# Feed-forward matrices as 2x2 blocks with seven products, in one layer of a hybrid encoder on one core

## The chip, the core and the metric

The kernel runs on one of the eight cores of a Trainium2 chip. A core has five engines that run side by side and are tied together by semaphores: TensorE (PE in the profile) multiplies matrices, with weight loads on a row of their own (PEld); VectorE (DVE) does elementwise work and reductions; ScalarE (ACT) does elementwise functions and casts; GpSimd (POOL) does elementwise work on SBUF only; SyncE (SP) here issues DMA transfers. SBUF is the memory on the core with 128 partitions, PSUM the accumulators that TensorE writes. The metric is the device time of one execution in microseconds, and the median over runs is compared.

## The reference, cut to what matters

One encoder layer on 512 tokens of width 2048, in float32: a normalised input projection that feeds two recurrent head groups, an output projection, cross-attention into 256 memory tokens, a feed-forward part with hidden width 8192, and a last normalisation. The change is in the feed-forward part:

```python
hn = _rmsnorm(h, norm_mlp[l])
h = h + jnp.square(jax.nn.relu(hn @ mlp_w_up[l])) @ mlp_w_down[l]
return _rmsnorm(h, norm_final)
```

`mlp_w_up` is 2048 x 8192 and `mlp_w_down` is 8192 x 2048.

## The kernel before, in words

Activations lie transposed in SBUF: a tile holds 128 features by 512 tokens, so the residual stream `h` is 16 tiles (`hres`). A matrix product is made of matmuls of a 128x128 block of weights against a 128x512 tile. To keep float32 precision every operand is cut into a rounded high part and the rest (`split`, L131 to L136: ScalarE casts the high part, VectorE subtracts it from the source for the low part), and each block costs three matmuls, high by high, high by low and low by high (`gemm`, L152 and L124). Weights come in pieces of 128x1024 (eight blocks, 512 KB) through `wload`: a raw tile of three (`wraw`), split into one of two pairs (`whi`, `wlo`).

The first stages (projections, recurrent heads, keys) are ordered by a planner in the kernel itself (L248); these lines the change does not touch. From the value projection on, the kernel is written in plain order, and the framework sets the order of instructions on each engine, inserts the semaphores and gives tiles their places. There follow the value stage (vp, vo), the output projection (op), the scores and softmax (sc), the attention product (at), which also adds into `hres` and makes the split, gain-scaled input of the feed-forward part (`nh_`, `nl_`, 32 tiles), and the feed-forward part itself.

This runs in eight rounds. A round makes eight 128-row tiles of the hidden activations: each is 16 blocks x 3 matmuls (48), read from PSUM by ScalarE (relu), multiplied by the normaliser `rstd` and squared by VectorE, and split into `uh`, `ul`. Then for each of the 16 output tiles 8 blocks x 3 matmuls (24) multiply the round's hidden tiles, and VectorE adds the result from PSUM to `hres` (L1340). So hidden activations never leave SBUF, and GpSimd has no part. At the end the residual is squared, summed and normalised, and written out.

Of the kernel before, what the change touches and what calls it, by code (L numbers as in the profile page):

```python
# [9 lines left out]
F32 = mybir.dt.float32  # L10
F32R = mybir.dt.float32r
AF = mybir.ActivationFunctionType
ALU = mybir.AluOpType
# [4 lines left out]
P = 128  # L18
T = 512
M = 256  # L20
KD = 16
# [52 lines left out]
def build(tc, I, out):  # L74
    nc = tc.nc
    V, S, GP, PE = nc.vector, nc.scalar, nc.gpsimd, nc.tensor
    es = ExitStack()

    pc = es.enter_context(tc.tile_pool(name="pc", bufs=1))
    pd = es.enter_context(tc.tile_pool(name="pd", bufs=1, space=DRAM))  # L80
    ps = es.enter_context(tc.tile_pool(name="ps", bufs=1, space=PSUM))
    pw = es.enter_context(tc.tile_pool(name="pw", bufs=1))
# [17 lines left out]
    def col(name, i=0):  # L100
        o, w = PRM[name]
        return prm[:, o + i:o + i + 1]
# [17 lines left out]
    def psb(nm, tag="mx", bufs=2):  # L120
        return tile_of(ps, [P, 512], F32, tag, nm, bufs)
# [4 lines left out]
    def rsq(o, x, scale, eps):  # L126
        S.activation(o, x, AF.Ln, bias=eps, scale=scale)
        S.activation(o, o, AF.Exp, scale=-0.5)

    def split(src, hi, lo, gain=None):  # L130
        if gain is None:  # L131
            S.copy(hi, src)  # L132
            V.tensor_tensor(out=lo, in0=src, in1=hi.bitcast(F32), op=ALU.subtract)  # L133
# [204 lines left out]
    def act_tile(nm, dt=F32R):  # L338
        return tile_of(pa, [P, 512], dt, "act", nm, 32)
# [5 lines left out]
    rstd = pc.tile([P, T], F32, name="rstd")  # L345
# [4 lines left out]
    cnt = [0]  # L350
# [25 lines left out]
    raws, halves, used = {}, {}, set()  # L376
# [31 lines left out]
    acc = tl("r")  # L408
# [759 lines left out]

    pm_cm.__exit__(None, None, None)
    pq_cm.__exit__(None, None, None)  # L1170
    pl = es.enter_context(tc.tile_pool(name="pl", bufs=1, reuse_waits="tile"))

    def btile(nm):
        return pl.tile([P, 512], F32R, tag="actb", name=nm, bufs=32)

    def sl2(w=512):
        cnt[0] += 1
        return pl.tile([P, 512], F32, tag="sl", name=f"sl{cnt[0]}", bufs=3)[:, 0:w]

    hres = [pl.tile([P, T], F32, tag=f"h{k}", name=f"h{k}", bufs=1) for k in range(16)]  # L1180

    oh, ol = [], []
    for n in range(KD):
        r = pl.tile([P, 512], F32, tag="slr", name=f"mx{n}", bufs=3)
        nc.sync.dma_start(r, mixd[n])
        hi, lo = btile(f"oh{n}"), btile(f"ol{n}")
# [54 lines left out]
    acc = pl.tile([P, T], F32, tag="acc", name="acc1", bufs=1)  # L1241
    hh_, hl_ = [], []
    for n in range(KD):
        xr = sl2()
# [16 lines left out]
    V.tensor_scalar(out=nrcol, in0=rcol, scalar1=-1.0, scalar2=None, op0=ALU.mult)  # L1261


    phi = [btile(f"phi{m}") for m in range(8)]
    plo = [btile(f"plo{m}") for m in range(8)]
    for g in range(2):
        pts = [psb(f"sc{g}_{t}", ("mm", "mm", "mg", "mg")[t]) for t in range(4)]
        for n2 in range(8):
            cnt[0] += 1
            raw = pw.tile([P, 1024], F32, tag="wraw", name=f"kqr{cnt[0]}", bufs=NWR)  # L1270
            for i in range(2):
                nc.sync.dma_start(raw[:, i * 512:(i + 1) * 512], KQd[2 * n2 + i][:, g * 512:(g + 1) * 512])
            wh = pw.tile([P, 1024], F32R, tag="whi", name=f"kqh{cnt[0]}", bufs=NWS)
            wl = pw.tile([P, 1024], F32R, tag="wlo", name=f"kql{cnt[0]}", bufs=NWS)
            split(raw, wh, wl)
            for i in range(2):
                n = 2 * n2 + i
                w1, w2 = wh[:, i * 512:(i + 1) * 512], wl[:, i * 512:(i + 1) * 512]
                for t in range(4):
                    a1, a2 = hh_[n][:, t * P:(t + 1) * P], hl_[n][:, t * P:(t + 1) * P]  # L1280
                    mm(pts[t], a1, w1, start=(n == 0), stop=False)
                    mm(pts[t], a1, w2, start=False, stop=False)
                    mm(pts[t], a2, w1, start=False, stop=(n == 15))
        ptr = [[None] * 2 for _ in range(2)]
        probs = []
        for t in range(4):
            for e in range(2):
                s = pts[t][:, e * M:(e + 1) * M]
                mx = pl.tile([P, 1], F32, tag="mx1", name=f"mx{g}_{t}_{e}", bufs=4)
# [3 lines left out]
                pr = pl.tile([P, 512], F32, tag="actb", name=f"pr{g}_{t}_{e}", bufs=32)[:, 0:M]  # L1293
                sm = pl.tile([P, 1], F32, tag="sm1", name=f"sm{g}_{t}_{e}", bufs=4)
                S.activation(pr, s, AF.Exp, bias=nb, scale=rcol[:, t:t + 1], accum_out=sm)
                V.reciprocal(out=sm, in_=sm)
                V.tensor_scalar(out=pr, in0=pr, scalar1=sm, scalar2=None, op0=ALU.mult)
                probs.append(pr)
        for e in range(2):
            for mt in range(2):  # L1300
                pt = psb(f"ptr{g}_{e}_{mt}")
                for t in range(4):
                    PE.transpose(pt[:, t * P:(t + 1) * P], probs[t * 2 + e][:, mt * P:(mt + 1) * P], ident)
                kk = (g * 2 + e) * 2 + mt
                S.copy(phi[kk], pt)
                V.tensor_tensor(out=plo[kk], in0=pt, in1=phi[kk].bitcast(F32), op=ALU.subtract)

    acc = pl.tile([P, T], F32, tag="acc", name="acc2", bufs=1)
    nh_, nl_ = [], []
    for n in range(KD):  # L1310
        pt = psb(f"at{n}", "mm", 2)
        gemm(pt, VOd[n // 4][:, :, (n % 4) * P:(n % 4 + 1) * P], 8, phi, plo)
        V.tensor_tensor(out=hres[n], in0=hres[n], in1=pt, op=ALU.add)
        hi, lo = act_tile(f"nh{n}"), act_tile(f"nl{n}")
        split(hres[n], hi, lo, col("norm_mlp", n))
        nh_.append(hi)
        nl_.append(lo)
        finish(n, acc)
    pt = psb("pss2")
    mm(pt, ones, acc)  # L1320
    rsq(rstd, pt, 1.0 / 2048, b_eps6)


    for e in range(8):
        uh, ul = [], []
        for i in range(8):
            pt = psb(f"up{e}_{i}", "mm", 2)
            gemm(pt, I["w_up"][e * 8 + i], KD, nh_, nl_)
            r = sl2()
            S.activation(r, pt, AF.Relu)  # L1330
            V.tensor_tensor(out=r, in0=r, in1=rstd, op=ALU.mult)
            V.tensor_tensor(out=r, in0=r, in1=r, op=ALU.mult)
            hi, lo = btile(f"uh{e}_{i}"), btile(f"ul{e}_{i}")
            split(r, hi, lo)
            uh.append(hi)
            ul.append(lo)
        for n in range(KD):
            pt = psb(f"dn{e}_{n}", "mm", 2)
            gemm(pt, I["w_dn"][e, n], 8, uh, ul)
            V.tensor_tensor(out=hres[n], in0=hres[n], in1=pt, op=ALU.add)  # L1340


    acc = pl.tile([P, T], F32, tag="acc", name="acc3", bufs=1)
    for n in range(KD):
        finish(n, acc)
    pt = psb("pss3")
# [10 lines left out]
def layout(inputs):  # L1357
# [28 lines left out]
    def put(name, arr, rows=slice(0, P)):  # L1386
        o, n = PRM[name]
        prm[rows, o:o + n] = arr
# [14 lines left out]
    for n, k in (("w0", "rwkv_w0"), ("a0", "rwkv_a0"), ("kk", "rwkv_k_k"), ("ka", "rwkv_k_a"),  # L1403
# [21 lines left out]
    d["w_up"] = tiles(a["mlp_w_up"][0])  # L1425
    wd = a["mlp_w_down"][0]
    d["w_dn"] = np.ascontiguousarray(
        wd.reshape(8, 8, P, 16, P).transpose(0, 3, 2, 1, 4).reshape(8, 16, P, 1024))
    return d


# [14 lines left out]
```

## Time and profile before

| | us |
|---|---|
| median of 3 runs (3126.75 to 3129.79) | 3126.99 |
| the profiled execution | 3125.39 |
| its span, first to last instruction | 3123.6 |
| up to the query-key fold, 0 to 1066 | 1066 |
| query-key fold (kq), value stage (vp, vo), 1066 to 1345 | 279 |
| output projection, scores, attention product, 1345 to 1703 | 358 |
| feed-forward part, 1703 to 3099 | 1396 |
| last normalisation and output, 3099 to 3124 | 25 |

In a group's row stand the line, the engine, the operation, output and inputs by the program's names, the shapes and the count; then busy time and mean nanoseconds of one, and the engine's idle time before them with what ended it. Matmuls are pipelined: a matmul's own duration (389 ns) is longer than the distance between two of them, so what a stage of matmuls costs is read from its length and their number. A line can be a helper's.

### The profile page before, as it was taken

To read this page: it belongs to the slowest core of one execution; us is meant where nothing else is said; L and a number is where in the kernel's file an instruction comes from. 1 tells how busy PE (TensorE), PEld (TensorE's weight loads), DVE (VectorE), ACT (ScalarE), POOL (GpSimd) and SP (SyncE) were. 2 spreads that over 40 slices of the span, in tenths; PEclk is the share of its full clock that TensorE was granted. 3 is DMA by queue.
4 is the path that set the end of the run, shared out by engine and by line. 5 is a ranking of instruction groups with operands and counts; after the bars stand their busy time and mean duration, and the time that the engine had idled before them with its cause. 6 is when DMAs were issued, how large, how long until landed. Compare 5 with 4: busy or idle time off the path is not lost.

```text
span 3123.6 us, 44560 instructions
## 1 busy us (share of the span) xinstructions
PE 3069.4 (98%) x18294; PEld 2529.6 (81%) x18294; DVE 1564.7 (50%) x2259; ACT 1192.9 (38%) x1568; POOL 202.5 (6%) x547
## 2 busy tenths in 40 slices
PE   8999999999999999999999999999999999999997
PEld 6878888888777898788878888888888888888885
DVE  6576666666667647434355433334333433333344
ACT  6455454454555555533244222222222222222232
POOL 0202311311311000000000000000000000000000
PEclk9999999999999999999999999999999999999998
DMA  5332423432434686853323332323333332323332
GB/s 172 105 85 78 107 80 82 110 82 80 131 88 146 192 278 218 263 174 118 105 88 95 100 96 95 99 97 95 98 98 95 99 98 95 99 97 95 99 97 95
DMA packets 203388, 360.79 MB, mean 116 GB/s; under 512 B 89064, under 2 KB 108780, under 8 KB 203184
## 3 DMA queue, kind: packets, MB, share of 16 engines
q1 hardware_dynamic: 198576, 349.55, 36.6%
q10 hardware_dynamic: 4608, 8.39, 0.7%
q8 instruction: 144, 2.36, 0.3%
q14 instruction: 60, 0.49, 0.1%
HBM read 327.06 MB, written 30.81 MB: 115 GB/s over the span
## 4 chain that ended last, share of the span: by engine, by line
PE 71%; DMA 1%; ACT 1%; DVE 1%; issue 0%; ACTq 0%; DVEq 0%; SPq 0%
PE dn L124 22%; PE up L124 22%; PE op L124 6%; PE py L248 3%; PE vo L124 3%; PE kq L248 3%; PE sc L124 3%; PE kp L248 3%; PE at L124 3%; PE vp L124 2%; DMA mx<-mixd 1%; DMA out_dram<-sl 0%; DMA wraw<-in_w_in 0%; PE rs L248 0%; PE gs L248 0%
## 5 line engine op out<-in xcount | busy, mean ns | idle before, releaser
L132 ACT CAST whi<-wraw 128x1024 fp32r<-128x1024 f32 x368 | 387.3, 1052 | 1098.0 <-PE dn L124 471.5
L133 DVE TENSOR_TENSOR wlo<-wraw,whi 128x1024 fp32r<-128x1024 f32 x368 | 450.8, 1225 | 533.7 <-ACT whi L132 532.9
L124 PE MATMUL dn<-ul,whi 128*128 128x512 f32 x1024 | 399.3, 390 | 0.0
L124 PE MATMUL up<-nl,whi 128*128 128x512 f32 x1024 | 398.8, 389 | 0.0
L124 PE MATMUL dn<-uh,wlo 128*128 128x512 f32 x1024 | 398.5, 389 | 0.0
L124 PE MATMUL dn<-uh,whi 128*128 128x512 f32 x1024 | 398.4, 389 | 0.0
L124 PE MATMUL up<-nh,whi 128*128 128x512 f32 x1024 | 398.4, 389 | 0.0
L124 PE MATMUL up<-nh,wlo 128*128 128x512 f32 x1024 | 398.4, 389 | 0.0
L248 PE MATMUL py<-xhi,whi 128*128 128x512 f32 x928 | 374.2, 403 | 13.2 <-ACT xhi L248 10.8
L248 PE MATMUL py<-xhi,wlo 128*128 128x512 f32 x928 | 371.9, 401 | 0.6 <-DVE wlo L248 0.5
L248 PE MATMUL py<-xlo,whi 128*128 128x512 f32 x928 | 371.9, 401 | 0.0
L1340 DVE TENSOR_TENSOR h<-h,dn 128x512 f32<-128x512 f32 x128 | 87.9, 687 | 400.6 <-PE dn L124 400.6
L248 DVE TENSOR_TENSOR wlo<-wraw,whi 128x1024 fp32r<-128x1024 f32 x180 | 221.6, 1231 | 132.7 <-ACT whi L248 127.8
L248 ACT CAST whi<-wraw 128x1024 fp32r<-128x1024 f32 x180 | 188.9, 1049 | 234.0 <-PE py L248 188.6
L124 PEld LDWEIGHTS dn<-ul,whi 128*128 128x128 f32 x1024 | 192.2, 188 | 42.9 <-DVE ul L133 2.9
L124 PEld LDWEIGHTS up<-nl,whi 128*128 128x128 f32 x1024 | 192.2, 188 | 40.2 <-issue 0.2
L124 PEld LDWEIGHTS up<-nh,whi 128*128 128x128 f32 x1024 | 192.2, 188 | 40.1
L124 PEld LDWEIGHTS dn<-uh,whi 128*128 128x128 f32 x1024 | 192.2, 188 | 39.9
L124 PEld LDWEIGHTS up<-nh,wlo 128*128 128x128 f32 x1024 | 192.2, 188 | 39.7 <-issue 0.2
L124 PEld LDWEIGHTS dn<-uh,wlo 128*128 128x128 f32 x1024 | 192.2, 188 | 39.5
L248 PEld LDWEIGHTS py<-xhi,whi 128*128 128x128 f32 x928 | 175.1, 189 | 52.6 <-ACT xhi L248 10.8
L248 PEld LDWEIGHTS py<-xhi,wlo 128*128 128x128 f32 x928 | 175.0, 189 | 37.7 <-DVE wlo L248 1.7
(678 smaller groups left out, 4808.6 us busy)
## 6 DMA issues: line engine op xcount, KB each, us to landing
wraw<-in_w_up SPq DMA_DIRECT2D x128, 512.0 KB, 3.6
wraw<-in_w_dn SPq DMA_DIRECT2D x128, 512.0 KB, 3.6
wraw<-in_w_in SPq DMA_DIRECT2D x118, 512.0 KB, 3.9
wraw<-in_wk SPq DMA_DIRECT2D x32, 512.0 KB, 3.7
wraw<-in_wqT SPq DMA_DIRECT2D x32, 512.0 KB, 3.9
wraw<-in_wv SPq DMA_DIRECT2D x32, 512.0 KB, 4.7
wraw<-in_wo SPq DMA_DIRECT2D x32, 512.0 KB, 3.6
wraw<-in_w_out SPq DMA_DIRECT2D x32, 512.0 KB, 3.9
```

The source lines that it names most:

```text
L124: PE.matmul(o, l, r, start=start, stop=stop)
L132: S.copy(hi, src)
L133: V.tensor_tensor(out=lo, in0=src, in1=hi.bitcast(F32), op=ALU.subtract)
L248: f(*a, **k)
L1340: V.tensor_tensor(out=hres[n], in0=hres[n], in1=pt, op=ALU.add)
```

## The change

Both feed-forward products are made by the scheme of Strassen in Winograd's form. A unit takes 256 output rows and a set of row groups (pairs of 128 input rows) and cuts weights and activations into 2x2 blocks: the weights into a11, a12, a21, a22 by halves of the output and of each input pair, the activations by halves of the pair and of the tokens (256 each). Instead of eight block products it makes seven (`product`), of these weight sides: a11; s1 = a21 + a22; s2 = s1 - a11; a11 - a21; a22; s4 = a12 - s2; a12. The activation sides are seven tiles per group (`comb`), each with its high part in columns 0 to 255 and its low part in 256 to 511, made by `place` with four subtractions on GpSimd, seven copies on ScalarE and seven subtractions on VectorE. The four weight sums of a unit are on GpSimd, the seven splits as before on ScalarE and VectorE, now of the sums too. Seven additions on VectorE put the PSUM results together in two output tiles (`c1`, `c2`, of the three `sl` tiles).

The up product has 32 units with all eight groups (blocks of 128x1024). Its outputs are scaled, clipped and squared (`square`) and written to device memory (`Ud`, 64 writes from ScalarE's queue). The down product is run after all of up, in one chunk of two groups and six chunks of five (blocks of 128x256 and 128x640), eight units each; the result of each unit is added to `hres` by GpSimd (`into`; by VectorE in the last unit). `unit` reads a group back from memory and rebuilds its seven tiles; this is placed among the units of the chunk before. The weights are laid out by block in the inputs.

Around it: pools are regrouped so that the 56 activation tiles fit, the attention stage builds the first ones in place of `nh_` and `nl_`, the softmax rows get tiles of their own, and the reloaded mixer outputs use `sl` tiles.

```diff
-        hi, lo = act_tile(f"nh{n}"), act_tile(f"nl{n}")
-        split(hres[n], hi, lo, col("norm_mlp", n))
+        g = sl2()
+        S.activation(g, hres[n], AF.Copy, scale=col("norm_mlp", n))
+        if n % 2 == 0:
+            ge = g
+        if n % 2 == 0 and n < KD - 2:
+            for i in (B11, T1):
+                place(i, n // 2, ge, None)
+        elif n % 2 == 1:
+            for i in range(2 if n < KD - 2 else 0, 7):
+                place(i, n // 2, ge, g)
...
+    def put(i, k, src):
+        t = comb[i][k]
+        S.copy(t[:, HA], src)
+        V.tensor_tensor(out=t[:, HB], in0=src, in1=t[:, HA].bitcast(F32), op=ALU.subtract)
+    def sub(o, a, b):
+        GP.tensor_tensor(out=o, in0=a, in1=b, op=ALU.subtract)
+    def place(i, k, e, o):
+        if i == T1:
+            sub(e[:, HA], e[:, HB], e[:, HA])
+        elif i == T2:
+            sub(e[:, HA], o[:, HB], e[:, HA])
...
+        put(i, k, o[:, HB] if i == B22 else o[:, HA] if i == B21 else e[:, HB] if i == T3 else e[:, HA])
...
+        def product(i, tag, a):
...
+            split(a, hi, lo)
+            pt = psb(f"{nm}_{i}", tag)[:, 0:M]
+            for z, k in enumerate(ks):
+                sl = slice(z * P, z * P + P)
+                mm(pt, hi[:, sl], comb[i][k][:, HA], start=z == 0, stop=False)
+                mm(pt, hi[:, sl], comb[i][k][:, HB], start=False, stop=False)
+            for z, k in enumerate(ks):
+                mm(pt, lo[:, z * P:z * P + P], comb[i][k][:, HA], start=False, stop=z == len(ks) - 1)
...
+        a11 = raw(pw, "wraw", NWR, 0)
+        a21 = raw(pw, "wraw", NWR, 1)
+        a22 = raw(pool[0], "wraw2", 3, 2)
+        a12 = raw(pool[0], "wraw2", 3, 3)
+        p1 = product(B11, "mx", a11)
...
+        S.copy(u1, p1)
+        s1 = raw(pool[0], "ws", 2, None)
+        GP.tensor_tensor(out=s1, in0=a21, in1=a22, op=ALU.add)
+        p5 = product(T1, "mg", s1)
+        s2 = raw(pool[0], "ws", 2, None)
+        sub(s2, s1, a11)
+        p6 = product(T2, "mm", s2)
...
+        add(u2, u1, p6)
+        add(u4, u2, p5)
+        sub(a21, a11, a21)
+        p7 = product(T3, "mm", a21)
+        add(u3, u2, p7)
+        add(c22, u3, p5)
+        done(1, HB, c2)
+        p4 = product(T4, "mx", a22)
+        add(c21, u3, p4, ALU.subtract)
+        done(1, HA, c2)
+        s4 = raw(pool[0], "ws", 2, None)
+        sub(s4, a12, s2)
+        p3 = product(B22, "mg", s4)
+        add(c12, u4, p3)
+        done(0, HB, c1)
+        p2 = product(B21, "mm", a12)
+        add(c11, u1, p2)
+        done(0, HA, c1)
...
-    for e in range(8):
...
-            gemm(pt, I["w_up"][e * 8 + i], KD, nh_, nl_)
...
-            gemm(pt, I["w_dn"][e, n], 8, uh, ul)
-            V.tensor_tensor(out=hres[n], in0=hres[n], in1=pt, op=ALU.add)
+    for p in range(32):
+        def square(i, half, c):
+            t = c[:, half]
+            V.scalar_tensor_tensor(out=t, in0=t, scalar=0.0, in1=rstd[:, half], op0=ALU.max, op1=ALU.mult)
+            S.activation(t, t, AF.Square)
+            if half is HA:
+                nc.scalar.dma_start(Ud[p][:, i, :], c)
+        strassen(f"up{p}", (pu, 1024), [I["w_up"][p, i] for i in range(4)], list(range(8)), square)
...
+    chunks = [(0, 2)] + [(2 + 5 * c, 7 + 5 * c) for c in range(6)]
...
+            def into(i, half, t):
+                h = hres[2 * n + i][:, half]
+                eng = V if c == 6 and n == 7 else GP
+                eng.tensor_tensor(out=h, in0=h, in1=t[:, half], op=ALU.add)
+            if c == 0 and n < 5:
+                unit(g1 + n)
+            if 0 < c < 6 and n in (1, 3, 5):
+                unit(g1 + n // 2)
...
+            strassen(f"dn{c}_{n}", (pv, 640), [src[i] for i in range(4)], [g % 8 for g in range(g0, g1)],
+                     into, used)
```

More of the change, by code (lines that the diff above doesn't have):

```diff
@@ L1239, in finish @@
             V.tensor_tensor(out=acc, in0=acc, in1=sq, op=ALU.add)
-    acc = pl.tile([P, T], F32, tag="acc", name="acc1", bufs=1)
+    acc = ph.tile([P, T], F32, tag="acc", name="acc1", bufs=1)
     hh_, hl_ = [], []
@@ L1261, in build @@
     V.tensor_scalar(out=nrcol, in0=rcol, scalar1=-1.0, scalar2=None, op0=ALU.mult)
-    phi = [btile(f"phi{m}") for m in range(8)]
-    plo = [btile(f"plo{m}") for m in range(8)]
+    prob = [btile(f"pr{m}", F32) for m in range(16)]
+    phi = [ctile(f"phi{m}") for m in range(8)]
+    plo = [(ctile if m < 2 else btile)(f"plo{m}") for m in range(8)]
     for g in range(2):
@@ L1306, in build, with alloc @@
                 V.tensor_tensor(out=plo[kk], in0=pt, in1=phi[kk].bitcast(F32), op=ALU.subtract)
-    acc = pl.tile([P, T], F32, tag="acc", name="acc2", bufs=1)
-    nh_, nl_ = [], []
+    HA, HB = slice(0, M), slice(M, 2 * M)
+    NT = 56
+    comb = [[None] * 8 for _ in range(7)]
+    def alloc(k):
+        for i in range(7):
+            made[0] += 1
+            comb[i][k] = (act_tile if made[0] <= 32 else btile)(f"cb{i}_{k}")
+    made = [0]
+    B11, T1, T2, T3, T4, B22, B21 = range(7)
+    def put(i, k, src):
+        t = comb[i][k]
+        S.copy(t[:, HA], src)
+        V.tensor_tensor(out=t[:, HB], in0=src, in1=t[:, HA].bitcast(F32), op=ALU.subtract)
@@ L1310, in build @@
+    acc = ph.tile([P, T], F32, tag="acc", name="acc2", bufs=1)
+    for k in range(7):
+        alloc(k)
     for n in range(KD):
@@ L1321, in build @@
     rsq(rstd, pt, 1.0 / 2048, b_eps6)
-    for e in range(8):
-        uh, ul = [], []
-        for i in range(8):
-            pt = psb(f"up{e}_{i}", "mm", 2)
-            gemm(pt, I["w_up"][e * 8 + i], KD, nh_, nl_)
[L1329 to L1338, printed above, removed]
-            gemm(pt, I["w_dn"][e, n], 8, uh, ul)
-            V.tensor_tensor(out=hres[n], in0=hres[n], in1=pt, op=ALU.add)
@@ L1343, in build @@
-    acc = pl.tile([P, T], F32, tag="acc", name="acc3", bufs=1)
+    pl_cm.__exit__(None, None, None)
+    Ud = [pd.tile([P, 2, 512], F32, name=f"ud{i}", tag=f"ud{i}") for i in range(32)]
+    pu_cm = tc.tile_pool(name="pu", bufs=1, reuse_waits="tile")
+    pu = pu_cm.__enter__()
+    for p in range(32):
[6 more added lines that the diff above has]
+        strassen(f"up{p}", (pu, 1024), [I["w_up"][p, i] for i in range(4)], list(range(8)), square)
@@ new lines, in build, with load, unit @@
+    pu_cm.__exit__(None, None, None)
+    pv = es.enter_context(tc.tile_pool(name="pv", bufs=1, reuse_waits="tile"))
+    def load(g, i):
+        t = pv.tile([P, 512], F32, tag="ur", name=f"ur{g}_{i}", bufs=4)
+        nc.sync.dma_start(t, Ud[g][:, i, :])
+        return t
+    def unit(g):
+        e, o = load(g, 0), load(g, 1)
+        for i in range(7):
+            place(i, g % 8, e, o)
+    chunks = [(0, 2)] + [(2 + 5 * c, 7 + 5 * c) for c in range(6)]
+    for g in range(2):
+        unit(g)
@@ new lines, in build, with used @@
+    for c, (g0, g1) in enumerate(chunks):
+        for n in range(8):
+            def into(i, half, t):
[6 more added lines that the diff above has]
+                unit(g1 + n // 2)
+            late = [(g, load(g, 0), load(g, 1)) for g in (g1 + 3, g1 + 4)] if 0 < c < 6 and n == 7 else []
+            def used(i):
+                for g, e, o in late:
+                    place(i, g % 8, e, o)
+            src = I["w_dn0"][n] if c == 0 else I["w_dn"][c - 1, n]
+            strassen(f"dn{c}_{n}", (pv, 640), [src[i] for i in range(4)], [g % 8 for g in range(g0, g1)],
+                     into, used)
@@ L1344, in build @@
+    acc = ph.tile([P, T], F32, tag="acc", name="acc3", bufs=1)
     for n in range(KD):
@@ L1424, in layout, with blocks7 @@
         wo.reshape(4, 4, P, 4, 512).transpose(3, 0, 2, 1, 4).reshape(4, 4, P, 2048))
-    d["w_up"] = tiles(a["mlp_w_up"][0])
+    def blocks7(w):
+        v = w.reshape(w.shape[0] // 256, 2, P, w.shape[1] // 256, 2, P)
+        t = [v[:, k, :, :, m].transpose(2, 1, 0, 3) for m, k in ((0, 0), (1, 0), (1, 1), (0, 1))]
+        return np.ascontiguousarray(np.stack(t, 1).reshape(w.shape[1] // 256, 4, P, -1))
+    d["w_up"] = blocks7(a["mlp_w_up"][0])
     wd = a["mlp_w_down"][0]
-    d["w_dn"] = np.ascontiguousarray(
-        wd.reshape(8, 8, P, 16, P).transpose(0, 3, 2, 1, 4).reshape(8, 16, P, 1024))
+    d["w_dn0"] = blocks7(wd[:512])
+    d["w_dn"] = np.stack([blocks7(wd[512 + 1280 * c:512 + 1280 * (c + 1)]) for c in range(6)])
     return d
```

49 lines of the change are left out of this document (39 added, 10 removed).

## The prediction

> **What bounds the kernel now.** I read the page's busy shares and slices, then the chain that ended last, then stages by window. Below are rows of the page, of the chain (start, length) and of two windows (length, then busy time of TensorE, its weight loads, VectorE, ScalarE and GpSimd, granted clock, share and GB/s of the DMA engines):
>
> ```profile
> PE 3069.4 (98%) x18294; PEld 2529.6 (81%) x18294; DVE 1564.7 (50%) x2259; ACT 1192.9 (38%) x1568; POOL 202.5 (6%) x547
> ...
> POOL 0202311311311000000000000000000000000000
> PEclk9999999999999999999999999999999999999998
> ```
> ```profile
> 1703.36 3.63 PE up L124 x16
> ...
> 1878.79 87.04 PE up L124 x384
> 1965.83 87.27 PE dn L124 x384
> ...
> 3011.83 87.29 PE dn L124 x384
> ```
> ```profile
> 1703.00:1791.00 88.00, 88.00 (x387) 72.30 (x386) 35.45 (x40) 29.54 (x36) 0.00 (x0) 1.00 0.30 96
> 1791.00:1878.00 87.00, 87.00 (x385) 71.74 (x384) 31.89 (x34) 17.96 (x18) 0.00 (x0) 1.00 0.30 96
> ```
>
> The feed-forward part begins at 1703.36 and ends at 3011.83 + 87.29 = 3099.12: 1395.8 us, eight times one up and one down stretch. TensorE is busy in all of it (87 of 87), VectorE for 32 to 35, ScalarE for 18 to 30, GpSimd never; the clock is 1.00. So the stage costs its matmuls: 87.04 us / 384 = 226.7 ns for each of 6144 matmuls of 512 columns, and nothing else matters there. The profiled run took 3125.39 us, 1.6 below the median of 3126.99; I sum against the profiled run. A change within 0.2% (6 us) is not told from none.
>
> **Matmuls.** Seven block products instead of eight, each over half the tokens: per matrix 32 x 8 x 7 x 3 = 5376 matmuls of 256 columns. Their price is in the stage that folds queries into keys:
>
> ```profile
> L248 PE MATMUL kq<-khi,whi x256: 278/283/284, 1066.2 to 1158.3; 128*128 128x256 f32 x128
> L248 PEld LDWEIGHTS kq<-klo,whi x256: 187/192/192, 1066.2 to 1158.3; 128*128 128x128 f32 x128
> ...
> L248 PE MATMUL kq<-khi,wlo x256: 277/283/314, 1066.4 to 1158.5; 128*128 128x256 f32 x128
> ```
>
> Three such groups of 256 run from 1066.2 to 1158.5: 92.3 us / 768 = 120 ns, slightly more than half of 226.7, although each loads weights for 188 to 192 ns beside it. So TensorE alone needs 5376 x 0.120 = 645 us per matrix, 1290 in all: 106 below now. That is all the change can bring.
>
> **The other engines.** Prices, by groups of equal shape (busy time and mean ns of one behind the first bar):
>
> ```profile
> L132 ACT CAST whi<-wraw 128x1024 fp32r<-128x1024 f32 x368 | 387.3, 1052 | 1098.0 <-PE dn L124 471.5 <-PE up L124 375.2 <-issue 141.4
> ...
> L1207 ACT COPY rstd<-vp 128x256 f32<-128x256 f32 x16 | 5.9, 372 | 20.8 <-PE vp L124 20.7
> ```
> ```profile
> L133 DVE TENSOR_TENSOR wlo<-wraw,whi 128x1024 fp32r<-128x1024 f32 x368 | 450.8, 1225 | 533.7 <-ACT whi L132 532.9
> ...
> L1208 DVE TENSOR_TENSOR sl<-vp,rstd 128x256 f32<-128x256 f32 x16 | 6.7, 422 | 11.3 <-ACT rstd L1207 11.3
> L248 DVE SCALAR_TENSOR_TENSOR mhl<-wraw,prm,mhl 128x256 fp32r<-128x256 f32 x16 | 6.7, 480 | 3.5 <-ACT mhl L248 3.5
> L133 DVE TENSOR_TENSOR vlo<-sl,vhi 128x256 fp32r<-128x256 f32 x16 | 6.7, 418 | 0.0
> ```
> ```profile
> L248 POOL TENSOR_TENSOR gEs<-gE,cst 128x512 f32<-128x512 f32 x8 | 10.3, 1292 | 2.2 <-ACT gE L248 2.2
> ...
> L248 POOL TENSOR_TENSOR sr<-sr,sr 64x64 f32<-64x64 f32 x8 | 2.5, 313 | 0.6
> ```
>
> VectorE grows by 1.05 ns a column (1225 at 1024, 418 at 256), so a 640-wide split costs 0.82 us. GpSimd grows by 979/448 = 2.19 ns: 0.73 us at 256, 1.57 at 640, 2.41 at 1024 (the last two are estimates beyond its widest row). ScalarE does seven casts a unit, 7 x 1.05 + 0.37 + four squares of about 0.4 = 9.4 of an up unit's 20.2 us: beside other work, priced at nothing; without that cover the casts are 7.4 us a unit.
>
> Can VectorE and GpSimd work side by side? Two places answer it:
>
> ```profile
> 114.95 0.69 DVE L248 TENSOR_TENSOR y<-py,rstd 128x512 f32<-128x512 f32 x1 [2.34 <-PE py L248]
> ...
> 115.27 0.23 POOL L248 TENSOR_TENSOR sr<-sr,sr 64x15 f32<-64x15 f32 x1
> ...
> 115.84 1.22 DVE L248 TENSOR_TENSOR wlo<-wraw,whi 128x1024 fp32r<-128x1024 f32 x1 [0.21 <-ACT whi L248]
> 115.87 1.30 POOL L248 TENSOR_TENSOR sr<-sr,sr 64x28 f32<-64x28 f32 x1
> ```
> ```profile
> 697.26 1.28 POOL L248 TENSOR_TENSOR gEs<-gE,cst 128x512 f32<-128x512 f32 x1
> 697.94 1.68 DVE L248 TENSOR_TENSOR wlo<-wraw,whi 128x1024 fp32r<-128x1024 f32 x1 [0.17 <-ACT whi L248]
> ```
>
> Beside a VectorE operation that reads PSUM (py) GpSimd keeps its 0.23 us. Beside a weight split, which reads two SBUF tiles, an operation of 0.23 takes 1.30 and ends at 117.17, just after the split (117.06). The other way round, a split that starts while GpSimd works takes 1.68 instead of 1.22, ending 1.08 after GpSimd's end. So VectorE's two-SBUF-input work and GpSimd's sums exclude each other. About 0.13 us of start-up lies beside the other's tail at each change of turn (117.17 - 0.23 is 0.12 before the split's end; 1.22 - 1.08 = 0.14). Call this taking turns. Today it costs the stage nothing, since GpSimd rests there.
>
> The Trainium skill, SBUF — State Buffer, section Who interferes with whom, has this pair of engines sharing a port as an exclusive lock, the loser fully blocked for the whole instruction. The rows agree on the exclusion and differ by the 0.13 us; taken at its word, the sums below stand without the deductions, which is the rival "whole lengths".
>
> **Up, one of 32 units.** TensorE 168 x 0.120 = 20.2. Turns: VectorE 7 splits x 1.225 + 4 scale-and-clip x 0.48 = 10.5; GpSimd 4 sums x 2.41 = 9.64; together 20.1, less 15 x 0.13 = 18.2. VectorE's 7 additions from PSUM (2.95) may lie beside GpSimd. Floor 20.2 (TensorE), ceiling with no overlap 10.5 + 2.95 + 9.64 = 23.1. One loop is longer than the floor. An output tile is written to memory before its slot of three is free, and in the built order the next unit's first addition waits for that with four splits behind it in VectorE's queue.
>
> ```profile
> wraw<-in_w_up SPq DMA_DIRECT2D x128, 512.0 KB, 3.6
> ...
> vod<-sl ACTq DMA_DIRECT2D x32, 256.0 KB, 5.3
> ```
>
> From the last addition: 0.42, split 1.23, scale 0.48, square 0.4, copy 0.37, landing 5.3 = 8.2. From the freed slot to the next last addition VectorE has 6 additions, 4 splits and 3 scalings (8.9) with two GpSimd turns between (4.8 - 0.5): 13.2. Sum 21.4, some of it overlapped by GpSimd: I take 21.0, 672 us for 32. Entry: two of the four weight blocks use space that the attention stage frees only at its end, so 3.6 of loading, then three sums (7.2) and a cast stand before the third product, against 5.8 us of matmuls: 7 to 9, I take 8.
>
> **Down.** 48 units of five row groups. TensorE 105 x 0.120 = 12.6. Turns: VectorE 7 x 0.82 = 5.8; GpSimd 4 x 1.57 + 4 additions into the residual x 0.73 = 9.2; together 15.0, less 15 x 0.13 = 13.0; ceiling, with VectorE's 2.95 of additions uncovered, 17.9. Walking through the built order, turns change at nearly every operation and about two thirds of the additions lie beside GpSimd, so near the floor: 13.9. Eight units of two groups: 5.0 of TensorE; turns 2.94 + 5.84 = 8.8, floor 6.8, ceiling 11.7; I take 7.5. Rebuilding the seven activation combinations, 32 times: 7 x 0.42 + 4 x 0.73 = 5.9, floor 4.4; three of GpSimd's four steps overwrite what VectorE just read and wait for ScalarE's copy (0.37) and VectorE's split, ceiling 8.2; I take 5.0. Sum 48 x 13.9 + 8 x 7.5 + 32 x 5.0 = 667 + 60 + 160 = 887. The reload of the activations at the start (landing about 3, then a combination) adds 8. Floor 624 + 54 + 141 = 819, ceiling 859 + 94 + 262 = 1215.
>
> **The rest.** SP's queue holds the weight loads in order, some waiting for GpSimd; they come half a unit early, so nothing, bounded by one landing (3.6) a stage. ScalarE issues 64 writes, two in each up unit, where it has some ten us free: nothing. In the attention stage the combinations are built beside 87 us of matmuls that leave room (turns of 9.7 in each 10.9): nothing, 10 at most. Moved pools: 0, within 3 either way. End: residual squares compete with a busy VectorE: 5.
>
> **Sum.** 672 + 8 + 887 + 8 + 5 = 1580 against 1395.8: +184. 3125.4 + 184 = 3310 us, slower by 6%.
>
> **Rivals.**
> - TensorE stays the bound and the change is faster: turns hide in slack, 645 + 645 + 21 of entries and end = 1311, 3040 us. The 106 us of saved matmuls speak for it; against it stand the blocked rows, by which the down floor alone (819) is over 645. It decides if the two engines hold each other up for under three quarters of their full down sum of 976 (48 x 15.0 + 8 x 8.8 + 32 x 5.9): up at 645 and down below 730 break even; my floor has 84%. Chance 0.12. The Trainium skill, TensorE: Matmul & The Clock Gate, section Back-to-back issue gap, gives columns over 2.4 plus 2.5 ns, 109 ns here, which would lower this rival by another 116 us; the row says 120 ns.
> - Whole lengths: no start-up is hidden. Up 20.1 + 1.9 of additions and waits = 22.0; down 15.9, 9.7 and 6.0: 704 + 1033 + 21 = 1758, 3490 us. For it: dependent operations wait for semaphores too. Against: 0.13 in both rows. Chance 0.14.
> - No overlap at all, the queues waiting in lockstep: 32 x 23.1 + 1215 + 21 = 1975, 3705 us. Against it: PSUM additions run free (0.23). Chance 0.06.
> - The change doesn't do what it says: the weight load (188 ns) bounds the 256-column matmul, 10752 x 0.188 = 2021, 3770 us. Against: 120 ns in the kq stage. Chance 0.02.
>
> **How the numbers follow.** Forecast 0.66, own range 3215 (up at 645, down floor, entries) to 3520. The four others leave 0.12 + 0.14 + 0.06 + 0.02. 3150 to 3520 takes in "whole lengths" and part of the way to the faster case, and leaves out 0.2. Slower 0.87, within 0.2% 0.02, faster 0.11.
>
> **What would show it.** Right: in the two stages TensorE's busy share falls below 95% in down, its waits end on the low split (or the high cast behind it); mean split time well over its clean value (1.225 in up, 0.82 in down); GpSimd's 1024-wide sums over 2.41 in the mean; up near 680 us, down near 895. Wrong: splits at their clean time beside GpSimd's sums, or TensorE gapless at 120 ns, or a GpSimd sum far from 2.2 ns a column. Forecast too low if TensorE pauses so long that its clock drops.

## The result, and the profile after

The changed kernel takes 3274.49 us (median of 4 runs, 3272.88 to 3275.31); the kernel before, beside it, 3127.39 (3126.75 to 3129.79). The ratio is 1.0468, 95% interval 1.045 to 1.0486: slower by 147 us. The profiled execution took 3274.63, its span 3272.9, 149.3 more than the span before.

The first fence is from the page: busy time by engine, then GpSimd and the granted TensorE clock in 40 slices. The second is the view by windows: length, then the busy time of TensorE, its weight loads, VectorE, ScalarE and GpSimd, granted clock, share and GB/s of the DMA engines. Its rows are all of up and the middle of down.

```profile
PE 3065.5 (94%) x22902; PEld 2733.5 (84%) x22902; DVE 2422.0 (74%) x3311; ACT 1517.6 (46%) x2296; POOL 1314.5 (40%) x1279
...
POOL 0211221231130000000025555555478888988884
PEclk9999999999999989999999999999979998998998
```
```profile
1730.00:2381.00 651.00, 648.36 (x5379) 647.43 (x5378) 592.51 (x579) 291.09 (x391) 345.30 (x130) 1.00 0.39 126
...
2480.00:3104.00 624.00, 543.60 (x4048) 524.77 (x4048) 561.42 (x694) 255.70 (x458) 542.89 (x397) 0.92 0.34 101
```

Up and down part ways. In up TensorE is busy for 648 of 651 us and the stage costs its matmuls: 648.36 / 5379 = 120.5 ns each, 20.2 us a unit. In down it is busy for 543.6 of 624, 87%, while VectorE (561) and GpSimd (543) are busy about nine tenths of the time; in that busy time is the time in which one is held up by the other. Set side by side, in us (stage limits by the first and last matmul of each stage):

| | before | after | difference |
|---|---|---|---|
| start of the feed-forward part | 1703.2 | 1724.1 | +20.9 |
| entry into up | 0 | 5.9 | +5.9 |
| up | 696 (eight stretches) | 651.0 | -45 |
| down | 700 (eight stretches) | 858.5 | +159 |
| from the last matmul of down to the end | 24.5 | 33.4 | +8.9 |

So half of the change gains its 45 us, the other half loses over three times as much, 6 us go at the entry, and 30 us are lost outside the feed-forward part. The groups of equal shape show what up and down are busy with (busy time and mean ns of one behind the first bar; of the 240 splits in the first row 112 belong to earlier stages, and the 128 of up take 1.98 us in the mean):

```profile
L133 DVE TENSOR_TENSOR wlo<-wraw,whi 128x1024 fp32r<-128x1024 f32 x240 | 390.8, 1628 | 139.2 <-ACT whi L132 137.6 <-PE up L124 0.2
L133 DVE TENSOR_TENSOR wlo<-wraw,whi 128x640 fp32r<-128x640 f32 x192 | 272.8, 1421 | 26.4 <-ACT whi L132 26.3
L1332 DVE TENSOR_TENSOR cb<-ur,cb 128x256 fp32r<-128x256 f32 x224 | 193.3, 895 | 31.1 <-ACT cb L1331 31.1
...
L1335 POOL TENSOR_TENSOR wraw<-wraw,wraw 128x1024 f32<-128x1024 f32 x32 | 104.0, 3249 | 2.4
...
L1335 POOL TENSOR_TENSOR ws<-ws,wraw 128x1024 f32<-128x1024 f32 x32 | 76.9, 2403 | 79.2 <-DVE wlo L133 78.0 <-DMA wraw<-in_w_up 1.2
L1335 POOL TENSOR_TENSOR ws<-ws,wraw 128x640 f32<-128x640 f32 x48 | 76.4, 1591 | 33.2 <-DVE wlo L133 33.2
```

A 640-wide split takes 1.42 us, a 256-wide one of the rebuilding 0.90, where 0.82 and 0.42 are their lengths undisturbed. GpSimd's 1024-wide sums take 2.40 where nothing is in their way and 3.25 in the sum a11 - a21, the 640-wide ones 1.59 at best. In a stretch of up the turns can be seen one by one (timeline: start, length, engine; in brackets the idle time before and what ended it):

```profile
2003.52 2.40 POOL L1392 TENSOR_TENSOR ws<-wraw,wraw 128x1024 f32<-128x1024 f32 x1 [1.21 <-DVE wlo L133]
...
2004.03 2.98 DVE L133 TENSOR_TENSOR wlo<-wraw,whi 128x1024 fp32r<-128x1024 f32 x1 [0.64 <-ACT whi L132]
...
2006.00 3.27 POOL L1335 TENSOR_TENSOR wraw<-wraw,wraw 128x1024 f32<-128x1024 f32 x1
...
2007.26 3.10 DVE L133 TENSOR_TENSOR wlo<-wraw,whi 128x1024 fp32r<-128x1024 f32 x1
```

GpSimd's first sum ends at 2005.92, the split that came during it at 2007.01, 1.09 later; the second sum ends at 2009.27, 2.26 after that split; the second split at 2010.36, again 1.09 later. Each is its own length (1.225, 2.40) less 0.14. In up TensorE's 20.2 us a unit cover this. In down they don't. The chain that ended last, in the last chunk (start, length, what), repeats itself each 13.2 us:

```profile
3164.12 0.74 ACT whi L132
3164.88 1.67 DVE wlo L133
...
3167.09 1.78 DVE wlo L133
...
3169.54 1.45 DVE wlo L133
...
3171.76 1.57 DVE wlo L133
3173.38 3.87 PE dn L124 x30
3177.27 0.74 ACT whi L132
```

In this chain VectorE's splits, drawn out to 1.45 to 1.78, stand between two stretches of TensorE. TensorE has other matmuls to do meanwhile: in such a plain unit, one without rebuilding, it is busy for 12.9 of 13.2 us, so a plain unit loses only 0.6 us against TensorE's 12.6. The long units are those in which activations are rebuilt. Windows of one plain unit and of two rebuilding units that stand at the same place of their chunks (limits by ScalarE's first copy from PSUM in each unit):

```profile
3176.15:3189.36 13.21, 12.94 (x108) 12.70 (x107) 11.84 (x14) 5.37 (x9) 12.29 (x9) 1.00 0.35 100
2631.19:2651.73 20.54, 16.09 (x98) 15.21 (x99) 20.27 (x25) 7.60 (x17) 16.51 (x14) 0.75 0.36 102
2894.85:2915.41 20.56, 14.30 (x98) 13.49 (x99) 20.29 (x25) 7.61 (x17) 16.53 (x14) 0.92 0.36 106
```

Fourteen wide units rebuild groups and take 20.5 to 23.2 us each; together they hold about 130 of the 214 us by which down is longer than TensorE's own 645. The first eight units, which carry five rebuilt groups, hold about 50 more. The last two rows also show what TensorE's clock does here: with 0.75 granted its matmuls take 16.1 us, with 0.92 they take 14.3, and the unit has the same length. So the lower clock only fills time in which TensorE would have waited.

In the waits of the feed-forward part TensorE waits 84.2 us for low splits and 29.6 for high casts, its weight loads 106.2 and 36.1 (much of it the same time):

```profile
PEld dn L124 <- DVE wlo L133: 106.2, 98, 4.4
...
PE dn L124 <- DVE wlo L133: 84.2, 88, 4.2
...
PE dn L124 <- ACT whi L132: 29.6, 23, 3.0
```

Nearly all of the 20.9 us ahead of the feed-forward part is lost in the value stage: vp runs from 1161.0 to 1274.8, 113.8 us against 95.5 before. The waits of the span name one long one, and the timeline shows its cause:

```profile
PE vp L124 <- DVE sl L1213: 19.7, 1, 19.7
```
```profile
1176.01 15.19 SPq L1190 DMA_DIRECT2D sl<-mixd  x10
...
1191.70 0.42 DVE L1213 TENSOR_TENSOR sl<-vp,rstd 128x256 f32<-128x256 f32 x1
...
1192.27 0.77 PE L124 MATMUL vp<-mhl,whi 128*128 128x512 f32 x1 [19.74 <-DVE sl L1213]
```

The sixteen mixer outputs are now reloaded into the three `sl` tiles, and the value tile (L1213) needs one of them too. In the built order all sixteen reloads stand ahead of it. Before, the reloads had three tiles of their own, and no wait in vp was longer than 1.2 us.

### The profile page after: what moved, and what is told of

Read it like the earlier page. It is cut to its first block, busy times and chain, and to the rows that moved or that the text cites. A ratio compares the mean times of both kernels' runs of the same rounds, so it can differ in the third digit from the quotient of the medians.

```text
span 3272.9 us, 57766 instructions
## 1 busy us (share of the span) xinstructions
PE 3065.5 (94%) x22902; PEld 2733.5 (84%) x22902; DVE 2422.0 (74%) x3311; ACT 1517.6 (46%) x2296; POOL 1314.5 (40%) x1279
## 5 line engine op out<-in xcount | busy, mean ns | idle before, releaser
L133 DVE TENSOR_TENSOR wlo<-wraw,whi 128x1024 fp32r<-128x1024 f32 (+2 forms) x464 | 686.1, 1479 | 165.7 <-ACT whi L132 163.9
L132 ACT CAST whi<-wraw 128x1024 fp32r<-128x1024 f32 (+2 forms) x464 | 404.1, 871 | 477.1 <-PE up L124 151.4
L124 PE MATMUL dn<-cb,whi 128*128 128x256 f32 x3584 | 535.8, 298 | 37.1 <-ACT whi L132 29.6
L124 PEld LDWEIGHTS dn<-cb,whi 128*128 128x128 f32 x3584 | 494.8, 206 | 45.2 <-ACT whi L132 36.1
L124 PE MATMUL up<-cb,whi 128*128 128x256 f32 x3584 | 468.9, 284 | 0.0
L124 PEld LDWEIGHTS up<-cb,whi 128*128 128x128 f32 x3584 | 447.9, 193 | 1.0 <-issue 0.5
L124 PE MATMUL dn<-cb,wlo 128*128 128x256 f32 x1792 | 308.9, 302 | 84.8 <-DVE wlo L133 84.2
L248 PE MATMUL py<-xhi,whi 128*128 128x512 f32 x928 | 375.0, 404 | 12.6 <-ACT xhi L248 10.5
L133 DVE TENSOR_TENSOR wlo<-ws,whi 128x640 fp32r<-128x640 f32 (+2 forms) x264 | 341.4, 1295 | 46.4 <-ACT whi L132 46.1
L124 PEld LDWEIGHTS dn<-cb,wlo 128*128 128x128 f32 x1792 | 257.1, 203 | 107.9 <-DVE wlo L133 106.2
L248 DVE TENSOR_TENSOR wlo<-wraw,whi 128x1024 fp32r<-128x1024 f32 x180 | 222.0, 1234 | 134.2 <-ACT whi L248 128.6
L248 ACT CAST whi<-wraw 128x1024 fp32r<-128x1024 f32 x180 | 188.9, 1050 | 235.8 <-PE py L248 188.7
```

The costliest lines, as they stand in the source:

```text
L124: PE.matmul(o, l, r, start=start, stop=stop)
L248: f(*a, **k)
```

## The experiments

My theory: the sums that GpSimd and VectorE make from SBUF exclude each other, so in down their lengths add up, and that sum, not TensorE, sets the unit. The rival: TensorE waits for something that the sums don't touch (landing weights, the order of the queues), and the long splits are only its shadow. The first four experiments and the first one on up alone were run once each, the others two to five times; runs of one kernel differed by 7 us at most (3074.99 to 3082.03).

**Sums of up issued twice.**

```diff
+        twice = 2 if w == 1024 else 1
+        for _ in range(2 * twice - 1):
+            GP.tensor_tensor(out=s1, in0=a21, in1=a22, op=ALU.add)
...
+        for _ in range(twice):
+            sub(s2, s1, a11)
...
+        for _ in range(twice):
+            sub(s4, a12, s2)
```

> In the up product each unit's GpSimd sums are issued eight times instead of four (s1 three times, s2 and s4 twice; the repeats write the same values). Theory, taking turns: VectorE's two-SBUF-input work (10.5 us a unit) and GpSimd's sums (now 19.3) exclude each other, less 0.13 at each of 19 turns: 27.3 us a unit instead of the 20.2 of the changed kernel, +227 us, about 3500 us in all, with the 1024-wide splits far above 1.225 us in the mean. Rival, each engine only keeps its own queue: GpSimd is busy 19.3 of 20.2 us, so the unit stays near 20.2 and the time near 3275 us.

3498.1 us, 224 above the changed kernel, or 7.0 for each of 32 units, which now take 27.2 us. Groups of this run:

```profile
L133 DVE TENSOR_TENSOR wlo<-wraw,whi 128x1024 fp32r<-128x1024 f32 x240 | 532.3, 2218 | 131.4 <-ACT whi L132 130.3
...
L133 DVE TENSOR_TENSOR wlo<-ws,whi 128x1024 fp32r<-128x1024 f32 x96 | 234.1, 2438 | 7.1 <-ACT whi L132 6.5
```

VectorE has the same work as in the changed kernel, yet its splits stretch to 2.22 and 2.44 us in the mean, from 1.63 and 1.68, and the unit follows the sum of turns: it is 0.1 off the expected 27.3.

**Weight sums of the wide down units replaced by constants** (same place, the same tiles written, nothing read).

```diff
+        def fill(o, a, b, op):
+            if w == 640:
+                for v in range(3):
+                    GP.memset(o, 0.01 * (v + 1))
+            else:
+                GP.tensor_tensor(out=o, in0=a, in1=b, op=op)
```

> In the 48 five-group units of the down product each of the four weight sums on GpSimd becomes three fills of the same tile with a constant (about 1.8 us together by the fill rows of before, against 1.57): GpSimd is no less busy, but reads nothing. The weight sums are left out, so the down product is not that of the reference. Taking turns (of reading GpSimd work only): 640-wide splits go back towards 0.82 us, turns fall to 7.3 us a unit and 11.7 with a rebuilt group, both under TensorE's 12.6, so a chunk of eight falls from 131.7 to about 101 us and the time to about 3115 us. Rival, GpSimd's occupancy or its queue delays the unit whatever it does: plain units stay at 13.2 us and the time near 3270 us.

3184.2 us: 90 below the changed kernel, 69 above what I expected. Plain units take 12.6 us, TensorE's own time, and down 769. GpSimd still writes these tiles, 271 us by the first row below (groups), and the split of the second row is nearly back at its clean 0.82. In the timeline behind it, the first pair is a fill beside a split, the second an addition beside a split:

```profile
L1383 POOL MEMSET ws<- 128x640 f32 x432 | 270.9, 634 | 38.4 <-DVE wlo L133 35.3
...
L133 DVE TENSOR_TENSOR wlo<-wraw,whi 128x640 fp32r<-128x640 f32 x192 | 173.0, 901 | 33.0 <-ACT whi L132 33.0
```
```profile
3079.42 0.82 DVE L133 TENSOR_TENSOR wlo<-wraw,whi 128x640 fp32r<-128x640 f32 x1
...
3079.51 0.64 POOL L1383 MEMSET wraw<- 128x640 f32 x1
...
3082.69 0.74 POOL L1484 TENSOR_TENSOR h<-h,sl 128x256 f32<-128x256 f32 x1
...
3083.02 1.09 DVE L133 TENSOR_TENSOR wlo<-wraw,whi 128x640 fp32r<-128x640 f32 x1
```

Both the fill and the split beside it keep their length; the split beside the addition takes 1.09 and ends 0.68 after it. So it is the sums' reading, not GpSimd being busy or late, that holds VectorE. A fill also waits for no weights, but that can't be what was gained: in the changed kernel GpSimd's weight sums waited only about 1 us in all for down's weights to land. (The Trainium skill, SBUF — State Buffer, section Who interferes with whom, says just this: VectorE work with two SBUF inputs contends with GpSimd work that reads SBUF, not with work that only writes it. These rows agree: 0.82 beside a fill, 1.09 beside an addition.) What I had overrated is how much of down hangs on the weight sums: units in which activations are rebuilt still take 16 to 19 us. There GpSimd's subtractions and residual additions (0.87 and 0.93 in the mean, 0.73 clean) go on taking turns with VectorE. Of the 214 us that down lies over TensorE's own 645 (48 x 12.6 + 8 x 5.0), 90 are the weight sums; 124 stay.

**Residual additions to VectorE.**

```diff
-                eng = V if c == 6 and n == 7 else GP
-                eng.tensor_tensor(out=h, in0=h, in1=t[:, half], op=ALU.add)
+                V.tensor_tensor(out=h, in0=h, in1=t[:, half], op=ALU.add)
```

> Only the four additions into the residual move from GpSimd to VectorE. Taking turns: four turns of 0.73 become four of 0.42 without a change of turn; plain unit 5.8 + 1.7 + 6.3 - 11 x 0.13 = 12.3, under TensorE's 12.6; a chunk of eight near 127 us instead of 131.7, the time near 3246 us. Rival, VectorE is full by its own work (busy 90% of the down stage): 1.7 us more a unit, about +80 us, 3355 us.

3281.5 us, where 3246 or 3355 was expected: no gain, and plain units still take 13.2 us, not the 12.6 that TensorE alone needs. Each addition costs 0.42 on VectorE instead of 0.73 on GpSimd, so the sum of turns falls, but the timeline of this run shows where it goes:

```profile
2686.82 1.57 POOL L1335 TENSOR_TENSOR ws<-ws,wraw 128x640 f32<-128x640 f32 x1 [0.76 <-DVE wlo L133]
...
2687.10 1.57 DVE L1476 TENSOR_TENSOR h<-h,sl 128x256 f32<-128x256 f32 x1
...
2688.92 0.81 DVE L133 TENSOR_TENSOR wlo<-wraw,whi 128x640 fp32r<-128x640 f32 x1
...
2689.79 0.86 PE L124 MATMUL dn<-cb,wlo 128*128 128x256 f32 x5 [0.36 <-DVE wlo L133]
```

An addition that nobody waits for comes 0.28 us into a sum of GpSimd, takes 1.57 instead of 0.42, and the split behind it in VectorE's queue comes late for TensorE. A sum of turns bounds a unit from below. Whether it is reached depends on which instruction stands in the queue when the other engine has the turn.

**All block sums on VectorE.**

```diff
-        GP.tensor_tensor(out=o, in0=a, in1=b, op=ALU.subtract)
+        V.tensor_tensor(out=o, in0=a, in1=b, op=ALU.subtract)
...
-        GP.tensor_tensor(out=s1, in0=a21, in1=a22, op=ALU.add)
+        V.tensor_tensor(out=s1, in0=a21, in1=a22, op=ALU.add)
...
-                eng = V if c == 6 and n == 7 else GP
-                eng.tensor_tensor(out=h, in0=h, in1=t[:, half], op=ALU.add)
+                V.tensor_tensor(out=h, in0=h, in1=t[:, half], op=ALU.add)
```

> All feed-forward work of GpSimd (weight sums, combinations, additions into the residual) moves to VectorE, GpSimd rests. Taking turns: since the two never worked side by side on SBUF pairs, little is lost: VectorE's sum is 18.3 us in an up unit (TensorE stays the bound at 20.2), 13.7 in a plain down unit (13.2 now), 4.6 for a rebuilt group (5.25 now): about 3295 us. Rival, GpSimd does work beside VectorE: its 9 to 12 us a down unit come on top of VectorE's, at least 5 us a unit, 3510 us or more.

3202.6 us: 72 below the changed kernel, and 92 below what I expected. One engine alone is faster than two that share the work. Rows of groups, and of the timeline:

```profile
L133 DVE TENSOR_TENSOR wlo<-wraw,whi 128x640 fp32r<-128x640 f32 x192 | 157.1, 818 | 14.2 <-PE dn L124 8.0 <-ACT whi L132 5.3
...
L1392 DVE TENSOR_TENSOR ws<-wraw,wraw 128x640 f32<-128x640 f32 x48 | 39.4, 820 | 5.3 <-DMA wraw<-in_w_dn 4.4 <-DVE wlo L133 0.2
```
```profile
3059.86 0.81 DVE L1392 TENSOR_TENSOR ws<-wraw,wraw 128x640 f32<-128x640 f32 x1
3060.60 0.81 DVE L133 TENSOR_TENSOR wlo<-ws,whi 128x640 fp32r<-128x640 f32 x1
3061.33 0.81 DVE L133 TENSOR_TENSOR wlo<-wraw,whi 128x640 fp32r<-128x640 f32 x1
```

A 640-wide sum costs 0.82 on VectorE and 1.59 on GpSimd. Where they can't run side by side, GpSimd's help costs twice what it relieves. (The Trainium skill, GPSIMD Engine Reference, section 4.1 Engine selection, puts elementwise work of two inputs at about two times slower on GpSimd; 1.59 to 0.82 agrees.) What I had missed in the expectation is in the second fence: instructions of 0.81 us start 0.735 apart. With 0.735 for each 640-wide and 0.335 for each 256-wide instruction, a plain unit has 11 x 0.735 + 11 x 0.335 = 11.8 us on VectorE, under TensorE's 12.6: the plain units of the last chunk take 12.6, those of up 20.2 (the first 20.9). A unit that carries 5/8 of a rebuilt group has 5/8 x 11 x 0.335 = 2.3 more, 14.1; measured, most take 13.8 to 14.6, as VectorE's sum says. Seven take 15.3 to 15.5. In all seven the granted clock is 0.89, in the shorter ones 1.00. Two units at the same place of their chunks:

```profile
2513.91:2529.36 15.45, 14.40 (x107) 14.40 (x108) 13.60 (x25) 6.66 (x10) 0.00 (x0) 0.89 0.34 99
2632.59:2646.56 13.97, 12.92 (x107) 12.92 (x108) 13.43 (x25) 6.68 (x11) 0.00 (x0) 1.00 0.36 107
```

VectorE's busy time differs by 0.17 us, TensorE's by 1.48, which is the whole difference of the two units. So here, with little waiting left, a lower granted clock costs time: about 10 us over the seven units. At the turn from one wide chunk to the next a unit takes about 20, and down 793 us, still over 90 longer than before the change.

**Mixer outputs into the residual's tiles**, which are unused until the output projection.

```diff
-        r = sl2()
+        r = hres[n]
         nc.sync.dma_start(r, mixd[n])
```

> The changed kernel with one edit: the sixteen reloaded mixer outputs land in the residual tiles (empty at that point) instead of the three sl tiles. Theory: the 20 us by which the attention product starts later (1634.4 against 1613.3) are one wait of the value stage for an sl tile behind the sixteen reloads; it goes, the vp stage ends near 1255 instead of 1275, and the time falls by 18 to 20 us to about 3255 us. Rival: the reloads themselves are late (kq ends 2 us later, DMA busy at 0.7), so the wait moves to the output projection or stays: 3270 to 3275 us.

3263.16 us (3261.76 to 3264.42, ratio 1.0433, 1.0416 to 1.045): 11 of some 20 us came back. vp takes 104.0 instead of 113.8 and 95.5. The timeline shows a new wait in place of the old:

```profile
1162.60 11.29 SPq L1190 DMA_DIRECT2D h<-mixd  x16
1174.29 40.88 SPq L152 DMA_DIRECT2D wraw<-in_wv  x14
...
1183.61 0.58 PE L124 MATMUL vp<-mhl,wlo 128*128 128x256 f32 x1 [8.10 <-DVE wlo L133]
```

With nothing to wait for, all sixteen reloads go in one burst, 11.3 us long on SP's queue, and the next weight load stands behind it. The three tiles of before had paced them: one to three reloads between two loads of weights.

**The same, each reload behind the value tile of its number.**

```diff
-    for n in range(KD):
+    def reload_mix(n):
         r = hres[n]
...
             vlo.append(l2)
+            reload_mix(n)
```

> The changed kernel with the mixer outputs reloaded into the tiles of the residual (as in the run with own tiles), and now each reload and its split written behind the value tile of the same number instead of all sixteen ahead of them. Theory: what the run with own tiles kept of the value stage's loss (8.1 us, one wait of TensorE for a low split in vp) is the burst of sixteen reloads on SP's queue, 11.3 us long, with the next weight load behind it; spread out, vp takes 95.5 us as before the change, so 3263 - 8 = 3255 us. Rival: the wait has another cause, such as the value tile's own chain, and vp keeps about 104 us: 3263 us.

3254.49 us, and vp runs from 1160.8 to 1255.4, 94.6 us. So the value stage's loss is accounted for: 20 us in all, of which 11 come back with tiles of their own and 9 more when the burst, which takes the old wait's place, is spread.

**Seven products for up alone**, down as before but for its input, which comes back from memory.

```diff
+    def reload(p):
+        raw = wraw()
+        nc.sync.dma_start(raw, Ud[p].rearrange("p a b -> p (a b)"))
...
+            split(raw[:, i * 512:(i + 1) * 512], hi, lo)
...
+            gemm(pt, I["w_dn"][e, n], 8, uh, ul)
+            V.tensor_tensor(out=hres[n], in0=hres[n], in1=pt, op=ALU.add)
```

> Seven products for the up matrix only, with its sums on GpSimd; the down matrix as in the kernel before (eight rounds of 512-column matmuls, eight products, GpSimd idle), its activations reloaded from memory and split. Theory: up gives its gain (651 us with 6 of entry, against 697), down costs 697 plus about 6 for the first reload, and the value stage's 20 us stay: 3127 - 46 + 6 + 6 + 20 = about 3113 us, faster than before. Rival, the loss is not in the down product's turns but comes with the 256-column scheme or the round trip through memory: no better than before, 3130 us or more.

3104.36 us, 23 under the kernel before, though the 20 us of the value stage are still lost in it. Windows of this run, up and down:

```profile
1730.00:2380.00 650.00, 647.34 (x5374) 646.67 (x5373) 591.74 (x586) 295.52 (x398) 344.29 (x128) 1.00 0.40 130
2381.00:3076.00 695.00, 695.00 (x3068) 575.48 (x3067) 285.58 (x326) 170.45 (x199) 0.00 (x0) 1.00 0.36 117
```

TensorE has no gap in down, and 2.7 us of gaps in up.

**Up alone, sums on VectorE, mixer outputs in the residual's tiles**: the block sums' part of the fourth edit and the whole fifth edit, on top of the last.

> As the kernel with seven products for up alone, and in addition the weight sums and combinations on VectorE and the mixer outputs in the residual tiles. Theory: up stays at TensorE's 20.2 us a unit (VectorE's own sum is 18.3) with a shorter entry, and no wait in the value stage: 3127 - 46 + 4 + 6 = about 3090 us, ratio near 0.988. Rival, VectorE too full in up (18.3 of 20.2) and late splits: units of 21 us or more, 3115 us or more.

3088.1 us (3086.54 to 3089.88), ratio 0.9874, 0.986 to 0.9889, as expected.

**The same with the reloads spread.**

> Seven products for up alone, sums on VectorE, mixer outputs in the residual's tiles, with each reload behind the value tile of the same number. Theory: the same 8 us come off as in the changed kernel with spread reloads: 3088 - 8 = 3080 us, 1.5% under the kernel before. Rival: the reloads now come too late for the output projection, which reads them right behind the value stage, and nothing is gained: 3088 us or more.

3077.06 us (3074.99 to 3082.03), ratio 0.9843, 0.9829 to 0.9856: 49.5 us, or 1.6%, faster than the kernel before. Up takes 647.8 (696 before), with 4.3 of entry, down 696.1; the feed-forward part again begins at 1702.4. GpSimd, as before the change, has no part in it, and VectorE is busy for 537 of 646 us in up:

```profile
1700.00:2346.00 646.00, 642.09 (x5320) 640.08 (x5319) 537.38 (x710) 292.22 (x395) 0.00 (x0) 1.00 0.39 131
```

Seven products for both matrices, with all sums on VectorE and the reloads spread, were not run together. An estimate from the two runs, 3202.6 less the 20 us of the value stage, is 3183 us, still slower than before the change.

## Why the prediction was right, and where its terms were off

The forecast was 3310 us; 3274.5 was measured, within its range, by the mechanism it named. Against the profiled execution, step by step in us:

| term | predicted | measured |
|---|---|---|
| up | 672 | 651.0 |
| entry | 8 | 5.9 |
| down, with its start | 895 | 858.5 |
| feed-forward part less 1395.8 | +179 | +119.6 |
| value stage (moved pools) | 0, within 3 | +20.9 |
| end | +5 | +8.9 |
| sum | +184 | +149.4 |

- *Matmuls of 256 columns at 120 ns*: right, 120.5 over the whole up stage. The rival by which weight loads bound them is out.
- *Taking turns, with 0.13 us hidden at each change*: right. The rows of up show 0.14, doubled sums lengthen the unit as computed (27.2 for 27.3), and fills, which read nothing, take no turn. One limit: without the residual additions on GpSimd the turns of a plain down unit sum to 12.3 and it still took 13.2, so there the sum is a lower bound and not the length. "Whole lengths" is out by the 0.14, "no overlap" with it.
- *Up at 21.0, because a slot of the output tiles comes free late*: wrong. I priced the landing of a write to `Ud` by another write of the same size, 5.3 us. It takes 2.0:

```profile
ud<-sl ACTq DMA_DIRECT2D x64, 256.0 KB, 2.0
```

  With 2.0 my loop of 21.4 is 18.1, below TensorE's 20.2, and up would have been 32 x 20.2 = 646, as measured within 5 (the first unit takes 22.2). So in up the rival "TensorE stays the bound" is what happened. Up also shows the limit of that cover: sums of twice the length break through it.
- *Down at 13.9 for a wide unit*: the size was off by 0.7, and 48 x 0.7 = 34 is nearly all of down's difference of 36.5. The rebuilt groups (0.3 too low each, 10 in all) and the eight small units with the start (13 too high) nearly cancel. The floor of 13.0 was the better number; the measured 13.2 lies beside it, in part by luck, since the run with fewer turns kept 13.2 too. *5.0 for a rebuilt group*: a chunk of eight units takes 131.9, less 8 x 13.2 leaves 26.3 for five, 5.3 each.
- *Moved pools and tiles at nothing*: this is the step that failed. I had counted the tiles and found them enough, but not walked through who asks for the shared three and in which order; a wait of 19.7 us came of it, 13% of the loss. With tiles of their own the reloads took nearly half of it back through SP's queue.
- *End at +5*: eleven of the sixteen squares of the residual are summed only after the last matmul, 8.6 us on VectorE, by the timeline:

```profile
3240.97 8.64 DVE L1244 TENSOR_TENSOR acc<-acc,sl 128x512 f32<-128x512 f32 x11
```

- *What would show it*: TensorE under 95% in down (87% in its middle), waits ending on the low split, splits over their clean time, sums over 2.41 in the mean: all seen. "Up near 680" and "down near 895" were not (651.0 and 858.5).
- *TensorE's clock*: its pauses do show in the granted clock, 0.92 in the middle of down against 1.00 in up. It did not lengthen the long units of down: rebuilding units at the same place of their chunks took 20.54 us at 0.75 and 20.56 at 0.92. Where the waits were mostly gone, in the run with all block sums on VectorE, it did cost time (15.45 at 0.89 against 13.97 at 1.00).

The errors went both ways, up and down 58 us too high, the value stage and the end 25 too low. That the second undoes nearly half of the first is luck. The sign rested on down alone, and there the floor was enough to tell it.

## What to carry to other kernels

When a change gives an idle GpSimd elementwise sums beside a VectorE that reads two SBUF tiles, add the two engines' times instead of taking the larger; at 1.59 against 0.82 us for the same sum, VectorE alone is the better place. Trade matmuls for elementwise work product by product: where a unit has 20.2 us of matmuls over 18 of sums it gains, where it has 12.6 over 13 and more it loses, and doing it in the first place only was worth 49.5 us here. And when buffers are regrouped, walk through the built order for each shared tag and for the DMA queue behind it: a tag of three can be a wait of 20 us, and it can also be what paces a queue.

## What the runs showed of the hardware that was not expected

- VectorE instructions that follow each other without a wait start closer than their length: 0.735 us apart at 0.81 (640 columns), 0.335 at 0.41 (256 columns).
- GpSimd's fills of 0.64 us run beside a two-input split without lengthening either (0.82), while an addition of 0.74 makes the split 1.09.
- Two kinds of writes of 256 KB to memory from the same queue land at different speed in the changed kernel: 5.3 us in the value stage (vo, 1275 to 1345), 2.0 in up. The DMA engines are busy for 0.82 of the first stretch and 0.39 of the second; whether that is the reason was not tried.
- Sixteen reloads of 256 KB issued in a row hold a weight load behind them on the same queue for 11.3 us, which cost TensorE one wait of 8.1; spread among the weight loads, they cost it none over 0.8.
- A lower granted clock left a unit with many waits of TensorE as long as it was (20.54 us at 0.75, 20.56 at 0.92) and lengthened one with few (15.45 at 0.89, 13.97 at 1.00).
